# A gated recurrence whose tiles hold both heads of one direction instead of both directions of one head

## The chip, the cores and the metric

The kernel runs on one core of one Trainium2 chip. The metric is the device time of one execution in microseconds (us); lower is better. The engines of a core work side by side, each on its own queue in order: TensorE (PE, with its weight loads shown as PEld), VectorE (DVE), ScalarE (ACT), GpSimd (POOL) and SyncE (SP), which issues most of the DMAs.

## What is computed

The reference is a stack of two two-layer transformer blocks over 512 tokens of width 1024, all in float32. The change touches one mixer of the second block alone, a gated linear recurrence (in both layers). For each of 6 heads with 64 keys and 64 values it runs forwards and backwards over the 512 tokens:

```
f = lb + (1 - lb) * sigmoid(z)          # one gate per key, per direction
k = (1 - lb) * sigmoid(-z)
state = f_t * state + k_t v_t           # forwards with z_fwd, backwards with z_bwd
o = q * state                           # o = o_fwd + o_bwd
```

The other mixers of those layers are a gated convolution of 31 taps and a dilated attention of 6 heads. After them come an output product and a convolutional feed-forward network.

## The kernel before, in words

Tokens lie along the free dimension and channels on the 128 partitions. Every large weight matrix comes in 128x1024 tiles by DMA and is split into a high and a low part (`weight`, L132: a cast on ACT, L129, and a subtraction on DVE, L130). A projection `proj` (L993) is 24 matmuls of 512 columns (`mm3`, L147 to L149) into a bank tagged `d`.

The kernel computes the recurrence without a scan over tokens, as a 512 x 512 matrix of scores for each head, built level by level. `LEVELS` (L937) are block lengths m = 1, 2, 4, ... 256. At level m, a key in one half of a block of 2m tokens meets a query in the other half. Forward scores have the query in the second half, backward scores in the first. Gates are gathered in products that double in length at each level.

In the kernel before, a tile of the recurrence belongs to one head: rows 0 to 63 hold the forward direction and rows 64 to 127 the backward one. There are a gate tile F, a key tile K and a query tile Q for each of the two heads of a pair p (three pairs in a layer). Per head and level:

- `queries` (L1149) multiplies queries by gates on DVE, once for each direction: 64 partitions x 256 elements, into a tile of 512 columns. The other half of the columns was set to zero when the layer began (L991), so that a product over 128 rows sums the two directions with nothing from the wrong half.
- `diagonal` (L1170) handles m up to 64 within 128 x 128 blocks. It makes 8 matmuls (128 rows, 64 output partitions, 64 columns) into one bank, tag `r`. The float32 matmul shows in the trace as two passes, so that 8 matmuls are 16 instructions. A masked copy on DVE (L1186) then picks this level's elements into `AD`; at m = 0 (the diagonal itself) a plain copy on ACT does (L1182), and at m = 64 two copies on ACT (L1189) into `AT`.
- `far` (L1196) handles m = 128 and 256, with 4 matmuls of 128 or 256 columns over 128 rows each, into two `r` tiles in turn, and copies on ACT (L1208, L1215).
- `double` (L1159) extends the products: K on DVE (L1167), then F on POOL (L1168), once for each direction, 64 partitions x 256 elements.

`recurrent` (L1218) runs the levels of the two heads one level apart: head 1 does level i - 1 while head 0 does level i, so there is one step more than there are levels. In pairs 1 and 2 each step also issues two taps of the convolution on DVE (L1022). After the levels come the products with the values (L1250, and L1257 and L1258 for the diagonal blocks, which use 64 rows and 64 output partitions each), a norm and a gate. `recurrent_start` (L1114) makes F, K and Q from the projections. It copies Q for each head and direction on ACT (L1139).

The eight banks of PSUM are `d` 2, `s` 2, `t` 2, `o` 1, `r` 1 (L1281). `s` and `t` belong to the dilated attention's scores and transposes (L328, L1091), `o` to its output and to that of the recurrence.

The steps are traced in the order `MIX_STEPS` (L1271): c0 r0 c1 d0 s1 r1 d1 s2 r2 e d2 (c convolution, r recurrence, d dilated attention, s the start of a recurrence, e the end of the convolution). A scheduler orders each engine's instructions when the program is built, earlier steps first. Later work fills the places where nothing earlier is ready; the order on the chip is then fixed.

Of the kernel before, what the change touches and what calls it, by code (L numbers as in the profile page):

```python
# [17 lines left out]
P = 128  # L18
D = 1024
KC = D // P  # L20
T = 512
# [948 lines left out]
def halves(ap, m):  # L970

    v = ap.rearrange("p (n two m) -> p n two m", two=2, m=m)
    return v[:, :, 0], v[:, :, 1]


class Mixers:


    def __init__(self, b, l, a, at, yp):
        self.b, self.l, self.a, self.at = b, l, a, at  # L980
        self.Y = [b.tile(yp, [P, T], F32, f"Y{k}") for k in range(KC)]
# [132 lines left out]
    def recurrent_start(self, p, pp, tag):  # L1114
# [3 lines left out]
        lb, om = b.lbs[self.l]  # L1118
        self.F, self.K, self.Q = [], [], []
        for h in range(2):  # L1120
            i = 2 * p + h
            pz = self.proj(16 + i)
# [9 lines left out]
        pq = self.proj(13 + p)  # L1132
        qp = b.tile(at, [P, T], F32, "raw")
        nc.scalar.activation(qp, pq, AF.Sigmoid)
        nc.vector.tensor_tensor(qp, qp, pq, op=ALU.mult)
# [12 lines left out]

    def queries(self, m, h):  # L1149
        b, Q, F = self.b, self.Q, self.F  # L1150
        nc = b.nc
        qs = self.qs[m]
# [6 lines left out]
    def double(self, m, h):  # L1159
# [10 lines left out]
    def diagonal(self, h, qs, m):  # L1170

        b, K, AT, AD = self.b, self.K, self.AT, self.AD
# [7 lines left out]
        src = pd.rearrange("p (a b) -> p a b", a=4)  # L1180
        if m == 0:
            nc.scalar.copy(AD[h], src)  # L1182
        elif m < 64:
            mk = b.recmask[:, int(math.log2(m))]
            mk = bass.AP(tensor=mk.tensor, offset=mk.offset, ap=[mk.ap[0], [0, 4], [1, 64]])
            nc.vector.copy_predicated(AD[h], mk, src)  # L1186
        else:
            for s in range(2):
                nc.scalar.copy(self.blocks(h, s, 1 - s), src[64 * s:64 * s + 64])  # L1189

# [4 lines left out]

    def far(self, m, h, qs):  # L1196
        b, K, AT = self.b, self.K, self.AT
        nc = b.nc
        for x in range(2):
            pf = b.tile(self.pp, [P, T], F32, "r")  # L1200
            if m == P:
                for y in range(2):
                    i = 2 * y + x
                    mm = nc.tensor.matmul(pf[:, y * P:(y + 1) * P], K[h][:, i * P:(i + 1) * P],
                                     qs[:, (i ^ 1) * P:((i ^ 1) + 1) * P], start=True, stop=True)
                for y in range(2):
                    i = 2 * y + x
                    nc.scalar.copy(AT[h][:, i, (i ^ 1) * P:((i ^ 1) + 1) * P], pf[:, y * P:(y + 1) * P])  # L1208
            else:
                u = slice(256 * (1 - x), 256 * (1 - x) + 256)  # L1210
                for y in range(2):
                    i = 2 * x + y
                    mm = nc.tensor.matmul(pf[:, 256 * y:256 * y + 256], K[h][:, i * P:(i + 1) * P], qs[:, u], start=True,
                                          stop=True)
                nc.scalar.copy(AT[h][:, 2 * x:2 * x + 2, u], pf.rearrange("p (y t) -> p y t", y=2))  # L1215
        return mm

    def recurrent(self, p):  # L1218
# [4 lines left out]
        self.AD = AD = [b.tile(at, [P, 4, 64], F32, "AD") for _ in range(2)]  # L1223
        for h in range(2):
            self.diagonal(h, self.Q[h], 0)
        levels = LEVELS[::-1]
        for i in range(len(levels) + 1):

            for h in range(2):
                if 0 <= i - h < len(levels):  # L1230
                    m = levels[i - h]
                    qs = self.queries(m, h)
                    if m < P:
                        self.diagonal(h, qs, m)
                    else:
# [39 lines left out]
def mixers(b, l, a, first, env):  # L1275
# [138 lines left out]
def layout(x):  # L1414
# [31 lines left out]

    v["lb_gamma"] = g("lb_gamma_2").reshape(2, 2, 6, 64).transpose(0, 2, 1, 3).reshape(-1)
    o["odd_w_in"] = wtiles(g("odd_w_in")[0])
# [4 lines left out]
    for l in range(2):  # L1453
# [3 lines left out]
        w = g("w_in_2")[l]  # L1457
        z = w[:, 2048:2816].reshape(D, 2, 6, 64).transpose(0, 2, 1, 3).reshape(D, 768)
        o[f"w_in_{l}"] = wtiles(np.concatenate([w[:, :2048], z, w[:, 2816:]], 1))
# [200 lines left out]
```

## Time and profile before

| | us |
|---|---|
| median of 3 runs | 3237.75 (3232.91 to 3242.60) |
| profiled execution, its own time | 3238.63 |
| profiled execution, span of its trace | 3236.6 |
| PE busy in the span | 3059.5 (95%) |
| DVE busy | 2131.1 (66%) |
| ACT busy | 1338.0 (41%) |
| POOL busy | 393.0 (12%) |

The span runs from the first instruction to the last. Busy time is the union of an engine's instructions. The matmuls are pipelined, so a busy PE is not necessarily at its peak. The granted clock of TensorE was 0.983 of full speed on average.

### The profile page before, as it was taken

What the parts mean: (1) busy time and instruction counts of PE and PEld (TensorE: products, weight loads), DVE (VectorE), ACT (ScalarE), POOL (GpSimd) and SP (SyncE); (2) the same over time, 40 slices, a digit from 0 to 9 for tenths busy, and PEclk for the clock granted to TensorE, in tenths of its full rate; (3) what the DMA queues carried; (4) which work ended last, traced back from release to release, by engine and by line L of the source; (5) the groups of instructions that cost most, each with busy time, mean ns of one, the idle gap of its engine ahead of it and who ended that gap; (6) DMA issues with size and microseconds to landing.
All of it is one profiled execution on the core that took longest, in us unless ns stands there. A gap on an engine that the chain in (4) does not pass through costs nothing.

```text
span 3236.6 us, 46233 instructions
## 1 busy us (share of the span) xinstructions
PE 3059.5 (95%) x18168; PEld 2509.2 (78%) x18168; DVE 2131.1 (66%) x3745; ACT 1338.0 (41%) x2343; POOL 393.0 (12%) x434
## 2 busy tenths in 40 slices
PE   7999999999999999899998889899999899899998
PEld 5776888888888777788887666688888666688887
DVE  6656565544457667556657997586766897764545
ACT  4656431221335555432334444542334345543423
POOL 0000100000021111200003332200002422210000
PEclk9999999999999999899999999999999999999999
DMA  6322324434302222156641222246652222323332
GB/s 235 101 75 86 131 86 124 130 124 124 110 22 77 53 59 79 66 163 189 188 156 53 71 74 66 92 134 189 191 176 66 71 80 66 105 74 96 98 96 61
DMA packets 100330, 342.65 MB, mean 106 GB/s; under 512 B 12176, under 2 KB 15888, under 8 KB 97040
## 3 DMA queue, kind: packets, MB, share of 16 engines
q1 hardware_dynamic: 93840, 325.53, 31.7%
q0 software_dynamic: 5120, 11.01, 1.6%
q8 instruction: 143, 2.34, 0.3%
q10 hardware_dynamic: 1152, 3.15, 0.3%
q14 instruction: 75, 0.61, 0.1%
HBM read 326.54 MB, written 2.10 MB: 102 GB/s over the span
## 4 chain that ended last, share of the span: by engine, by line
PE 46%; DVE 15%; ACT 2%; DMA 2%; issue 2%; POOL 0%; DVEq 0%; POOLq 0%; ACTq 0%; SPq 0%
PE dd L148 11%; PE dd L147 11%; PE dd L149 11%; DVE qs L1155 3%; DVE rk L1167 2%; PE d L148 2%; PE d L147 2%; PE d L149 2%; DVE wlo L130 1%; DMA K<-K 1%; PE o L1098 1%; DVE AD L1186 1%; DVE nw L242 1%; DMA wraw<-in_w_ada 1%; PE o L1250 1%
## 5 line engine op out<-in xcount | busy, mean ns | idle before, releaser
L148 PE MATMUL dd<-axl,whi 128*128 128x512 f32 (+1 forms) x2728 | 979.4, 360 | 12.7 <-DVE axl L244 11.3
L147 PE MATMUL dd<-axh,whi 128*128 128x512 f32 (+1 forms) x2728 | 978.9, 360 | 12.6 <-ACT axh L243 12.3
L149 PE MATMUL dd<-axh,wlo 128*128 128x512 f32 (+1 forms) x2728 | 976.9, 359 | 0.0
L129 ACT CAST whi<-wraw 128x1024 fp32r<-128x1024 f32 (+1 forms) x388 | 402.8, 1042 | 1010.7 <-PE dd L148 747.5
L130 DVE TENSOR_TENSOR wlo<-wraw,whi 128x1024 fp32r<-128x1024 f32 (+1 forms) x361 | 444.2, 1234 | 335.8 <-ACT whi L129 326.3
L148 PEld LDWEIGHTS dd<-axl,whi 128*128 128x128 f32 x2728 | 520.2, 191 | 92.1 <-DVE axl L244 14.2
L147 PEld LDWEIGHTS dd<-axh,whi 128*128 128x128 f32 x2728 | 519.9, 191 | 90.5 <-ACT axh L243 14.6
L149 PEld LDWEIGHTS dd<-axh,wlo 128*128 128x128 f32 x2728 | 520.4, 191 | 76.5
L218 POOL TENSOR_TENSOR sq<-sq,sq 128x256 f32<-128x256 f32 x90 | 73.0, 819 | 1851.7 <-ACT sq L213 1788.2
L181 DVE CUSTOM_DVE_ANT_0 adaj<-wraw,cond,vecs 128x1024 bf16<-128x1024 f32 x160 | 205.3, 1283 | 136.5 <-DMA wraw<-in_ada_w 87.1
L147 PE MATMUL d<-axh,whi 128*128 128x512 f32 x664 | 275.3, 415 | 12.0 <-ACT axh L129 9.8
L148 PE MATMUL d<-axl,whi 128*128 128x512 f32 x664 | 273.1, 411 | 1.8 <-DVE axl L130 1.8
L149 PE MATMUL d<-axh,wlo 128*128 128x512 f32 x664 | 270.8, 408 | 1.1 <-DVE wlo L130 1.1
L1168 POOL TENSOR_TENSOR rf<-rf 64x256 f32<-64x256 f32 x192 | 160.4, 835 | 388.2 <-DVE rk L1167 357.1
L154 DVE SCALAR_TENSOR_TENSOR hx<-dd,mod,hx 128x512 f32<-128x512 f32 (+1 forms) x113 | 72.7, 645 | 164.8 <-PE dd L149 164.7
L147 PE MATMUL dd<-ach,whi 128*128 128x256 f32 x568 | 160.7, 283 | 0.0
L148 PE MATMUL dd<-acl,whi 128*128 128x256 f32 x568 | 160.6, 283 | 0.0
L149 PE MATMUL dd<-ach,wlo 128*128 128x256 f32 x568 | 160.5, 282 | 0.0
L147 PEld LDWEIGHTS d<-axh,whi 128*128 128x128 f32 x664 | 126.2, 190 | 41.0 <-ACT axh L129 11.4
L148 PEld LDWEIGHTS d<-axl,whi 128*128 128x128 f32 x664 | 126.3, 190 | 31.6 <-issue 4.9
L149 PEld LDWEIGHTS d<-axh,wlo 128*128 128x128 f32 x664 | 126.4, 190 | 27.5 <-DVE wlo L130 2.3
L328 PE MATMUL s<-K,Q 128*128 128x256 f32 (+1 forms) x336 | 116.4, 357 | 21.8 <-DMA K<-K 13.6
(364 smaller groups left out, 4691.2 us busy)
## 6 DMA issues: line engine op xcount, KB each, us to landing
wraw<-in_mlp_w SPq DMA_DIRECT2D x128, 512.0 KB, 3.5
wraw<-in_w_ada SPq DMA_DIRECT2D x96, 512.0 KB, 4.0
wraw<-in_w_up SPq DMA_DIRECT2D x88, 512.0 KB, 3.5
wraw<-in_w_in SPq DMA_DIRECT2D x56, 512.0 KB, 3.5
wraw<-in_ada_w SPq DMA_DIRECT2D x48, 512.0 KB, 3.6
adaw<-in_ada_wb SPq DMA_DIRECT2D x16, 1024.0 KB, 4.8
wraw<-in_w_down SPq DMA_DIRECT2D x32, 512.0 KB, 3.6
wraw<-in_odd_w_in SPq DMA_DIRECT2D x24, 512.0 KB, 3.6
```

The lines of the kernel that those rows point to most:

```text
L129: self.nc.scalar.copy(hi, src)
L130: (e or self.nc.vector).tensor_tensor(lo, src, f32(hi), op=ALU.subtract)
L147: mm(ps, hi[:, k], xh[:, sl], start=first, stop=False)
L148: mm(ps, hi[:, k], xl[:, sl], start=False, stop=False)
L149: mm(ps, lo[:, k], xh[:, sl], start=False, stop=last)
L154: self.nc.vector.scalar_tensor_tensor(h, ps, gate[:, m:m + 1], h, op0=ALU.mult, op1=ALU.add)
L181: nc.vector.tensor_tensor_reduce(junk, raw, c, 1.0, self.vec(bias)[:, i:i + 1], ALU.mult, ALU.add, out[:, i:i + 1])
L218: e.tensor_tensor(acc, acc, s2, op=ALU.add)
L328: mm(ps, q[:, slot, toks], k1[:, keys], start=True, stop=False)
L1155: nc.vector.tensor_tensor(halves(qs[r], m)[1 - d], halves(Q[h][r], m)[1 - d], halves(F[h][r], m)[1 - d], op=ALU.mult)
L1167: nc.vector.tensor_tensor(k[d], k[d], whole[1 - d], op=ALU.mult)
L1168: nc.gpsimd.tensor_tensor(f[1 - d], f[1 - d], whole[d], op=ALU.mult)
```

## The change

A tile of the recurrence now belongs to one direction d: rows 0 to 63 are head 0, rows 64 to 127 head 1. Queries and doubling are done for both heads at once on 128 partitions. A query tile holds, for each direction, only the 256 columns that have queries, so there is nothing to zero and the tiles for the levels go. Each head's scores come from 64 rows of the array, one product per direction, with the two heads' products next to each other in two banks (`r` and `s`, and at m = 256 also `t` and `o`). At m = 1 to 32 a product has 32 columns. The two heads are no longer one level apart. The projection's output needs no copying to make Q. The weights' columns are reordered on the host.

```diff
-        self.qs = {m: b.tile(at, [P, T], F32, f"qs{m}") for m in LEVELS[::-1]}
-        for qs in self.qs.values():
-            b.nc.gpsimd.memset(qs, 0.0)
...
-        for h in range(2):
-            q = b.tile(at, [P, T], F32, "rq")
-            for d in range(2):
-                nc.scalar.copy(q[64 * d:64 * d + 64], qp[64 * h:64 * h + 64])
-            self.Q.append(q)
+        self.Q = b.tile(at, [P, T], F32, "rq")
+        nc.scalar.activation(self.Q, pq, AF.Sigmoid)
+        nc.vector.tensor_tensor(self.Q, self.Q, pq, op=ALU.mult)
...
+    def queries(self, m):
+        b, nc = self.b, self.b.nc
+        qs = b.tile(self.at, [P, 2, T // 2], F32, "qs")
         for d in range(2):
-            r = slice(64 * d, 64 * d + 64)
-            nc.vector.tensor_tensor(halves(qs[r], m)[1 - d], halves(Q[h][r], m)[1 - d], halves(F[h][r], m)[1 - d],
-                                    op=ALU.mult)
+            o = qs[:, d].rearrange("p (n m) -> p n m", m=m)
+            nc.vector.tensor_tensor(o, halves(self.Q, m)[1 - d], halves(self.F[d], m)[1 - d], op=ALU.mult)
         return qs
...
         for d in range(2):
-            r = slice(64 * d, 64 * d + 64)
-            f, k = halves(self.F[h][r], m), halves(self.K[h][r], m)
+            f, k = halves(self.F[d], m), halves(self.K[d], m)
             e = slice(m - 1, m) if d == 0 else slice(0, 1)
-            whole = [f[i][:, :, e].broadcast_to([64, n, m]) for i in range(2)]
+            whole = [f[i][:, :, e].broadcast_to([P, n, m]) for i in range(2)]
             nc.vector.tensor_tensor(k[d], k[d], whole[1 - d], op=ALU.mult)
             nc.gpsimd.tensor_tensor(f[1 - d], f[1 - d], whole[d], op=ALU.mult)
...
-        pd = b.tile(self.pp, [P, T], F32, "r")[:, :256]
+        pds = [b.tile(self.pp, [P, T], F32, t)[:, :256] for t in "rs"]
+        rows = [slice(64 * h, 64 * h + 64) for h in range(2)]
...
         for i in range(4):
-            for s in range(2):
-                k, q = i * P + 64 * s, i * P + 64 * (1 - s if m == 64 else s)
-                nc.tensor.matmul(pd[64 * s:64 * s + 64, 64 * i:64 * i + 64], K[h][:, k:k + 64], qs[:, q:q + 64], start=True,
-                                 stop=True)
+            for d in range(2):
+                for s in range(2):
+                    k = slice(i * P + 64 * s, i * P + 64 * s + 64)
+                    for h, r in enumerate(rows):
+                        out = pds[h][64 * s:64 * s + 64, 64 * i:64 * i + 64]
+                        if m == 0:
+                            nc.tensor.matmul(out, K[d][r, k], qs[r, k], start=d == 0, stop=d == 1)
+                        else:
+                            o = halves(out, m)[1 - d]
+                            q = qs[r, d, 64 * i + 32 * s:64 * i + 32 * s + 32].rearrange("p (n m) -> p n m", m=m)
+                            nc.tensor.matmul(o, K[d][r, k], q, start=True, stop=True)
...
+        if m == P:
+            pfs = [b.tile(self.pp, [P, T], F32, t) for t in "rs"]
...
+        else:
+            for d in range(2):
+                pfs = [b.tile(self.pp, [P, T], F32, t) for t in ("rs", "to")[d]]
...
-        for i in range(len(levels) + 1):
-
-            for h in range(2):
-                if 0 <= i - h < len(levels):
-                    m = levels[i - h]
-                    qs = self.queries(m, h)
-                    if m < P:
-                        self.diagonal(h, qs, m)
-                    else:
-                        last = self.far(m, h, qs)
-                    if 2 * m < T:
-                        self.double(m, h)
+        self.diagonal(self.Q, 0)
+        for m in LEVELS[::-1]:
+            qs = self.queries(m)
+            if m < P:
+                self.diagonal(qs, m)
+            else:
+                last = self.far(qs, m)
+            if 2 * m < T:
+                self.double(m)
             self.tap(2 if p else 0)
...
-                   "rf": 2, "rk": 2, "rq": 2, "AD": 2, "rg": 1, "nr0": 1, "nt": 1,
+                   "rf": 2, "rk": 2, "rq": 1, "qs": 3, "AD": 2, "rg": 1, "nr0": 1, "nt": 1,
```

At m = 64 the new `diagonal` makes 16 matmuls of 64 columns for both heads and the copies as before. At m = 128 `far` makes 8 matmuls of 128 columns over 64 rows and 4 copies (2 blocks each) in place of 8 of one block. At m = 256 it makes 8 matmuls of 256 columns over 64 rows and the 4 copies as before.

## Rows read from the trace of the kernel before

**Rows 1.** The page: the chain that ended last, by engine.

```profile
PE 46%; DVE 15%; ACT 2%; DMA 2%; issue 2%; POOL 0%; DVEq 0%; POOLq 0%; ACTq 0%; SPq 0%
```

**Rows 2.** Busy time by stretch: the first layer's three recurrences (first; sum).

```profile
1773.90:1838.30 64.40, 54.45 (x435) 40.29 (x435) 60.45 (x105) 19.09 (x35) 30.24 (x36) 0.98 0.20 58
...
sum 193.10, PE 163.67 PEld 117.97 DVE 179.59 ACT 70.55 POOL 86.51; mean PE 54.56 PEld 39.32 DVE 59.86 ACT 23.52 POOL 28.84
```

**Rows 3.** The same, second layer (2522:2586, 2629:2695, 2723:2788).

```profile
sum 195.00, PE 165.36 PEld 118.57 DVE 181.75 ACT 72.45 POOL 86.50; mean PE 55.12 PEld 39.52 DVE 60.58 ACT 24.15 POOL 28.83
```

**Rows 4.** The chain of waits, 1773 to 1840 us: by line.

```profile
by line: DVE qs L1155 27.7%; DVE rk L1167 18.9%; issue 8.2%; DVE cy L1022 8.0%; DVE AD L1186 6.8%; DVE wlo L130 6.1%; PE r L1213 4.2%; POOL rf L1168 3.6%; PE r L1178 2.8%; DVE Q L303 2.5%; DVE K L311 2.4%; PE o L1250 1.9%; PE d L149 1.7%; P
```

**Rows 5.** The timeline of DVE, 1784 to 1793 us: start, length, what.

```profile
1785.31 2.38 DVE L1155 TENSOR_TENSOR qs<-rq,rf 64x256 f32<-64x256 f32 x4
...
1788.33 0.44 DVE L1186 COPY_PREDICATED AD<-recmask,r 128x256 f32<-128x256 uint8 x1
1788.66 0.86 DVE L1167 TENSOR_TENSOR rk<-rk,rf 64x256 f32<-64x256 f32 x2
1789.55 1.64 DVE L130 TENSOR_TENSOR wlo<-wraw,whi 128x1024 fp32r<-128x1024 f32 x1
...
1792.55 0.72 DVE L1155 TENSOR_TENSOR qs<-rq,rf 64x256 f32<-64x256 f32 x1
```

**Rows 6.** Groups by line and shape: count, busy us, mean ns, idle before.

```profile
L130 DVE TENSOR_TENSOR wlo<-wraw,whi 128x1024 fp32r<-128x1024 f32 x345 | 429.0, 1246 | 320.9 <-ACT whi L129 311.4
...
L1168 POOL TENSOR_TENSOR rf<-rf 64x256 f32<-64x256 f32 x192 | 160.4, 835 | 388.2 <-DVE rk L1167 357.1 <-DVE st L1078 14.8 <-DVE st L1080 8.9
...
L218 POOL TENSOR_TENSOR sq<-sq,sq 128x256 f32<-128x256 f32 x90 | 73.0, 819 | 1851.7 <-ACT sq L213 1788.2 <-DMA cond<-in_c 58.6 <-DMA wraw<-in_w_up 3.7
...
L1139 ACT COPY rq<-raw 64x512 f32<-64x512 f32 x24 | 14.8, 619 | 7.1 <-DVE raw L1135 6.8
L218 DVE TENSOR_TENSOR sq<-sq,sq 128x256 f32<-128x256 f32 x36 | 16.3, 453 | 11.7 <-ACT sq L213 10.9
```

**Rows 7.** Line L1155: ns min/median/max, starts, shape.

```profile
L1155 DVE TENSOR_TENSOR qs<-rq,rf x216: 407/423/843, 1763.1 to 2784.8; 64x256 f32<-64x256 f32 x108
```

**Rows 8.** Busy sums of Rows 2's stretches: L1155; L1167; tile r; tile pr.

```profile
sum 193.10, DVE 57.66; mean DVE 19.22
...
sum 193.10, DVE 42.33; mean DVE 14.11
...
sum 193.10, PE 53.91 PEld 42.02 DVE 15.91 ACT 17.05; mean PE 17.97 PEld 14.01 DVE 5.30 ACT 5.68
...
sum 193.10, PE 5.13 PEld 3.40 DVE 14.82 ACT 9.69; mean PE 1.71 PEld 1.14 DVE 4.94 ACT 3.23
```

**Rows 9.** The timeline of PE, 1788.3 to 1791 us: around one burst.

```profile
1788.59 0.39 PE L147 MATMUL d<-axh,whi 128*128 128x512 f32 x1
1788.81 0.40 PE L148 MATMUL d<-axl,whi 128*128 128x512 f32 x1
1789.14 0.69 PE L1178 MATMUL r<-qs,rk 128*64 128x64 f32 x16
1789.75 0.50 PE L149 MATMUL d<-axh,wlo 128*128 128x512 f32 x1
```

**Rows 10.** The timeline of PE, 1842 to 1846 us: tiles of 64 rows.

```profile
1842.88 0.27 PE L1257 MATMUL o<-AD,rV 64*64 64x64 f32 x1
...
1843.36 0.22 PE L1258 MATMUL r<-AD,rV 64*64 64x64 f32 x1
```

**Rows 11.** The timeline of PE, 1820 to 1839 us: the far levels.

```profile
1820.98 0.68 PE L1204 MATMUL r<-qs,rk 128*128 128x128 f32 x4 [0.92 <-DVE qs L1155]
...
1825.64 1.02 PE L1213 MATMUL r<-qs,rk 128*128 128x256 f32 x4
...
1834.88 1.10 PE L1213 MATMUL r<-qs,rk 128*128 128x256 f32 x4 [2.94 <-DVE qs L1155]
```

**Rows 12.** Busy sum outside Rows 2: 1838.3:1882, 1945.7:1975.3, 2040.3:2065.

```profile
sum 98.00, PE 91.95 PEld 63.87 DVE 73.22 ACT 68.53 POOL 0.00; mean PE 30.65 PEld 21.29 DVE 24.41 ACT 22.84 POOL 0.00
```

More of the change, by code (lines that the diff above doesn't have):

```diff
@@ L1118, in recurrent_start @@
         lb, om = b.lbs[self.l]
-        self.F, self.K, self.Q = [], [], []
-        for h in range(2):
-            i = 2 * p + h
+        self.F, self.K = [], []
+        for d in range(2):
+            i = 2 * p + d
             pz = self.proj(16 + i)
@@ L1145, in recurrent_start, with double @@
         b.values(pp, self.V, raw, 4, tag)
[L1149 to L1152, printed above, removed]
+    def queries(self, m):
+        b, nc = self.b, self.b.nc
+        qs = b.tile(self.at, [P, 2, T // 2], F32, "qs")
         for d in range(2):
[L1154 to L1156 removed]
+            o = qs[:, d].rearrange("p (n m) -> p n m", m=m)
+            nc.vector.tensor_tensor(o, halves(self.Q, m)[1 - d], halves(self.F[d], m)[1 - d], op=ALU.mult)
         return qs
[L1159 removed]
+    def double(self, m):
         nc = self.b.nc
@@ new lines, in diagonal @@
+        rows = [slice(64 * h, 64 * h + 64) for h in range(2)]
+        if m == 64:
+            for i in range(4):
+                for s in range(2):
+                    for h, r in enumerate(rows):
+                        nc.tensor.matmul(pds[h][64 * s:64 * s + 64, 64 * i:64 * i + 64],
+                                         K[s][r, i * P + 64 * s:i * P + 64 * s + 64], qs[r, s, 64 * i:64 * i + 64],
+                                         start=True, stop=True)
+            for h in range(2):
+                src = pds[h].rearrange("p (a b) -> p a b", a=4)
+                for s in range(2):
+                    nc.scalar.copy(self.blocks(h, s, 1 - s), src[64 * s:64 * s + 64])
+            return
@@ new lines, in diagonal @@
+        for i in range(4):
+            for d in range(2):
+                for s in range(2):
+                    k = slice(i * P + 64 * s, i * P + 64 * s + 64)
+                    for h, r in enumerate(rows):
+                        out = pds[h][64 * s:64 * s + 64, 64 * i:64 * i + 64]
[5 more added lines that the diff above has]
+                            nc.tensor.matmul(o, K[d][r, k], q, start=True, stop=True)
@@ L1191, in blocks @@
+        for h in range(2):
+            src = pds[h].rearrange("p (a b) -> p a b", a=4)
+            if m == 0:
+                nc.scalar.copy(AD[h], src)
+            else:
+                mk = b.recmask[:, int(math.log2(m))]
+                mk = bass.AP(tensor=mk.tensor, offset=mk.offset, ap=[mk.ap[0], [0, 4], [1, 64]])
+                nc.vector.copy_predicated(AD[h], mk, src)
     def blocks(self, h, s, c):
@@ L1194, in blocks, with far @@
         return bass.AP(tensor=v.tensor, offset=v.offset + 64 * c, ap=[v.ap[0], [T + P, 4], [1, 64]])
-    def far(self, m, h, qs):
+    def far(self, qs, m):
         b, K, AT = self.b, self.K, self.AT
         nc = b.nc
-        for x in range(2):
-            pf = b.tile(self.pp, [P, T], F32, "r")
-            if m == P:
+        rows = [slice(64 * h, 64 * h + 64) for h in range(2)]
+        if m == P:
+            pfs = [b.tile(self.pp, [P, T], F32, t) for t in "rs"]
+            for d in range(2):
@@ L1202, in far @@
                 for y in range(2):
-                    i = 2 * y + x
-                    mm = nc.tensor.matmul(pf[:, y * P:(y + 1) * P], K[h][:, i * P:(i + 1) * P],
-                                     qs[:, (i ^ 1) * P:((i ^ 1) + 1) * P], start=True, stop=True)
-                for y in range(2):
[L1207 to L1215, printed above, removed]
+                    i = 2 * y + d
@@ new lines, in far @@
+                    for h, r in enumerate(rows):
+                        mm = nc.tensor.matmul(pfs[h][:, (2 * d + y) * P:(2 * d + y + 1) * P], K[d][r, i * P:(i + 1) * P],
+                                              qs[r, d, y * P:(y + 1) * P], start=True, stop=True)
+            for h in range(2):
+                for d in range(2):
+                    v = AT[h].rearrange("p a b -> p (a b)")
+                    v = bass.AP(tensor=v.tensor, offset=v.offset + d * T + (1 - d) * P,
+                                ap=[v.ap[0], [2 * (T + P), 2], [1, P]])
+                    nc.scalar.copy(v, pfs[h][:, 2 * d * P:2 * (d + 1) * P].rearrange("p (y q) -> p y q", y=2))
+        else:
+            for d in range(2):
+                pfs = [b.tile(self.pp, [P, T], F32, t) for t in ("rs", "to")[d]]
+                for y in range(2):
+                    i = 2 * d + y
+                    for h, r in enumerate(rows):
+                        mm = nc.tensor.matmul(pfs[h][:, 256 * y:256 * y + 256], K[d][r, i * P:(i + 1) * P], qs[r, d],
+                                              start=True, stop=True)
+                for h in range(2):
+                    nc.scalar.copy(AT[h][:, 2 * d:2 * d + 2, 256 * (1 - d):256 * (1 - d) + 256],
+                                   pfs[h].rearrange("p (y t) -> p y t", y=2))
@@ L1223, in recurrent @@
         self.AD = AD = [b.tile(at, [P, 4, 64], F32, "AD") for _ in range(2)]
-        for h in range(2):
-            self.diagonal(h, self.Q[h], 0)
-        levels = LEVELS[::-1]
-        for i in range(len(levels) + 1):
-            for h in range(2):
-                if 0 <= i - h < len(levels):
-                    m = levels[i - h]
-                    qs = self.queries(m, h)
-                    if m < P:
-                        self.diagonal(h, qs, m)
-                    else:
-                        last = self.far(m, h, qs)
-                    if 2 * m < T:
-                        self.double(m, h)
+        self.diagonal(self.Q, 0)
[3 more added lines that the diff above has]
+                self.diagonal(qs, m)
+            else:
+                last = self.far(qs, m)
+            if 2 * m < T:
+                self.double(m)
             self.tap(2 if p else 0)
```

20 lines of the change are left out of this document (4 added, 16 removed).

## The prediction, made before the change was run

> **What bounds the kernel now.** I began with the whole page: PE holds 46% of the chain that ended last and DVE only 15% [rows 1]. That average mixes stages, so I cut the trace into the stretches in which a recurrence runs. The first layer has three, 193.1 us in all. DVE is busy in 179.6 us of it (93%), PE in 163.7 us (85%) [rows 2]; the second layer shows the same, 181.8 of 195.0 us [rows 3]. In the first stretch the chain of waits runs over DVE: the queries hold 27.7% of it, the keys' doubling 18.9%, the masked copies 6.8%; the recurrence's matmuls hold about 6% [rows 4]. So these 388 us of the kernel hang on DVE. PE's far levels even wait for the queries, once for 2.94 us [rows 11].
>
> One level of both heads shows how the time is made up. From one group of queries to the next are 7.24 us (1785.31 to 1792.55), and DVE hardly pauses: four queries 2.38 us, two masked copies of 0.44, four doublings in two pairs of 0.86, and work from outside the recurrence, here a weight split of 1.64 us [rows 5]. The mean is 64.4 us / 9 levels = 7.15 us with all that surrounds them [rows 2].
>
> **What the change takes from DVE and POOL.** Queries and doublings go from four instructions of 64 partitions a level to two of 128. Partitions cost nothing: an addition on DVE over 128 x 256 takes 453 ns, the doubling on POOL over 64 x 256 835 ns and a POOL addition over 128 x 256 819 ns [rows 6]. The work therefore halves. Per layer 57.7 us of queries and 42.3 us of doubling [rows 8] lose 28.8 + 21.2 = 50.0 us of DVE time, 100 us in both layers. POOL's doubling loses 80 of 160.4 us [rows 6]. The ACT copies of Q, 14.8 us in 24 instructions [rows 6], go; four of the six starts lie in mid-mixer, where I count two of the four copies each as on the path: 4 x 2 x 0.62 = 5 us. POOL's zeroing at the layers' starts lies beside the norm before, and I count nothing for it; without that cover it would be worth some us more.
>
> **What it does to PE.** A burst of 16 passes (8 float32 matmuls) takes 0.69 us, the last pass itself 0.22: 31 ns a pass [rows 9]. The two heads make 32 passes a level, 1.0 us. Products of 64 rows and 64 output partitions stand already in the kernel: 32 passes of 64 columns start within 0.48 us, 15 ns a pass [rows 10], so four quarters of the array do run side by side. After the change a level m = 1 to 32 has 64 passes of 32 columns, a shape that the trace doesn't show. Bounds: 7.5 ns a pass if it goes by columns (0.5 us a level), 31 ns if the row halves don't overlap (2.0 us). I take the 64-column price of the nearest row, 15.5 ns: 1.0 us, no gain. The Trainium skill's TensorEngine Tiling (Array Packing), Instruction Overhead, has a rule against halving the columns: some 60 cycles of overhead a matmul, so that short products cost as those of 60 columns. By that rule the term is 1.0 us a level, by columns alone 0.5; no run here shows 32 columns yet.
>
> The rest of PE, per recurrence: m = 0 has 64 passes, 1.0 us as now. m = 64 has 32 passes, 0.5 for 1.0 us. At m = 128 sixteen passes of 135 ns ((0.68 - 0.27) / 3, [rows 11]) become sixteen half-height ones, in pairs 1.1 for 2.2 us. At m = 256, 214 ns a pass ((1.02 - 0.38) / 3, [rows 11]), 1.7 for 3.4 us. Sum now 1 + 7 + 2.2 + 3.4 = 13.6, after 1 + 6 + 0.5 + 1.1 + 1.7 = 10.3 us: 3.3 us less. A burst costs about 0.1 us going in (0.33 between starts where 0.22 is usual) and as much coming out [rows 9]. Sixteen bursts become eight and two or three in the far levels: 1 us less. Together some 4 us of PE a recurrence, 25 us in all, but PE is not what a phase waits for, so it counts as room for other work.
>
> **The level after the change.** With one group for both heads, no second head covers the first's waits. Adding up the chain: last query 0.42 [rows 7]; 0.1 to PE (estimate); the end of a running matmul and the switch 0.3 [rows 9]; 64 passes, 1.0 + 0.22 [rows 10]; two masked copies, 0.33 apart, 0.7 [rows 5]; first doubling 0.43 and 0.12 to POOL; two POOL instructions, 1.6 to 1.7 [rows 6]; 0.1 back to DVE. That is 5.1 us. DVE's work a level is 0.7 + 0.86 + 1.19 = 2.75 us, and the outside work of about 2 us that now runs in a level (7.15 x 0.93 - 4.8) makes 4.75. Chain and work are close, and an outside instruction that has just begun holds the chain up; I add half of one (0.5 us) and take 5.6 us. A phase is then 2.5 (m = 0) + 8 x 5.6 + 4.5 (m = 256, no doubling behind it; both ends are estimates from the same pieces) = 51.8 against 64.4 us: 12.6 us less, six times 76 us. The step that the stagger adds goes with it.
>
> **What is given back.** In a layer's phases PE has 163.7 - 53.9 = 109.8 us of other work [rows 2, 8]. In 155 us, at the same share and with 40 us for the recurrence, it finds 92; at 95% it finds 107. So 3 to 18 us move out, to stretches where PE reads 92.0 busy of 98.0 us [rows 12]. I take 9 us a layer. The new score tiles also take a bank of tag `s` at each level and `t` and `o` at the last. The dilated attention, which now runs its softmax inside the phases of pairs 1 and 2 (14.8 us of DVE and 5.1 of PE a layer on tile pr, [rows 8]), may have to wait for them. What is late next is then its transposes and its sum behind the recurrence. Nothing to 15 us a layer; I take 4, as the recurrence holds the bank only until the masked copy. New waits on the query tile cost nothing: three buffers, and a level reads one.
>
> **Sum.** 76 + 5 - 2 x 9 - 2 x 4 = 55 us off the profiled execution's own 3238.6 us (span 3236.6, 2 us around it, and 0.9 us over the median): 3184 us.
>
> **Rivals.** (a) *DVE and POOL hinder each other, and it remains.* A query alone takes 0.42 us, beside POOL 0.72, at most 0.84 [rows 5, 7]; a weight split 1.64 where the mean is 1.25 [rows 5, 6]. In the new level DVE has only outside work while POOL doubles. If that work is kept out of those 1.6 us, only the other 1.6 us (PE's burst and the switch) is left for 2.0 us of it, and each level grows by 0.4 us: 6 x 8 x 0.4 = 19 us, 3203 us. SBUF — State Buffer (Trainium skill), Who interferes with whom, states a harder form: a DVE instruction with two SBUF inputs and a GpSimd one that reads SBUF exclude each other for the whole instruction. By that rule the added time goes to the remaining POOL time; the rows' stretch of 0.3 to 0.4 us, less than POOL's 0.8, only partly bears it out.
>
> (b) *Full relief.* Phases stay as full of DVE as now and nothing moves out: (193.1 - 129.6 / 0.93) = 54 us a layer, with 5 us for Q: 3238.6 - 108 - 5 = 3126 us. For it speaks the 93%; against it the chain of 5.1 us.
>
> (c) *It doesn't do what it says:* the halves don't run side by side. Then a level has 2.0 us of passes: 6 x 1.0 + 1.0 + 0.5 + 1.1 + 1.7 = 10.3 us a recurrence in the chain, 62 us: 3246 us, no change. Rows 10 speak against.
>
> (d) *Slower: the unstaggered chain.* The orders on DVE and PE are fixed; if at each level the chain stands behind a whole weight split on DVE (1.64 us) and PE's waits last some 0.8 us more, a level is 5.1 + 1.6 + 0.8 = 7.5 us, and a phase 2.5 + 60 + 4.5 = 67 us, 2.6 more than now. No PE work moves out then, but the dilated attention's 8 us stay, and the 5 for Q: 3239 + 6 x 2.6 + 8 - 5 = 3258 us. It decides from a level of about (64.4 - 7) / 8 = 7.2 us on. For it: PE waits now for the queries although a second head runs; against: DVE's work a level falls to 4.75 us.
>
> **How the numbers follow.** Forecast 0.50 (own range 3150 to 3215), (a) 0.13, (b) 0.15, (c) 0.08, (d) 0.14. The range takes in (b) and (c), with the bound of 7.5 ns a pass (18 us less) and of the work moved out: 3115 to 3252; (d) stays out. A change under 0.3% (10 us) can't be told from none here. Faster: nearly all of the forecast, of (a) and of (b), 0.76; within 0.3%: most of (c) and a little of the others, 0.10; slower 0.14.
>
> **What would show it.** In the trace after: 108 queries and 96 doublings on DVE at about 0.42 to 0.6 us, POOL's about 0.8. The starts of successive query groups lie 5 to 6 us apart, and the six phases last about 52 us each. The bursts of 64 passes take about 1.2 us. DVE's share in the phases falls below 93%, and the stretches outside them grow by 10 to 15 us a layer. It is wrong if a level still takes over 7 us, if bursts take over 2 us, or if dilated scores first start after the last level and the tail grows by what the phases lost.

## The result, and the profile after

The changed kernel takes 3179.4 us (median of 4 runs, 3177.9 to 3180.5) against 3238.2 us before (median of 4 runs): a ratio of 0.9823, 95% interval 0.9809 to 0.9837, or 59 us less. 3184 us was forecast. The profiled execution's span is 3178.1 us against 3236.6.

The page after, its PE, DVE, ACT and POOL line and the chain by engine, answers to [rows 1]:

```profile
PE 3041.3 (96%) x19512; PEld 2500.7 (79%) x19512; DVE 2005.8 (63%) x3541; ACT 1313.7 (41%) x2292; POOL 293.8 (9%) x320
...
PE 49%; DVE 11%; DMA 3%; ACT 2%; issue 2%; POOL 1%; DVEq 0%; POOLq 0%; ACTq 0%; SPq 0%
```

DVE fell from 2131 to 2006 us of busy time, POOL from 393 to 294, PE from 3060 to 3041. In the chain DVE went from 15% to 11% and PE from 46% to 49%.

Where the time went is seen by stretches. Here are the three recurrences of the first layer (columns: stretch, length, busy us of PE, PEld, DVE, ACT and POOL with their instructions, granted clock, share of the DMA engines, GB/s). They answer to [rows 2]. The first begins with head 0's burst of m = 1; its m = 0 and head 1's burst of m = 1 had run before (1763 to 1767 us). The first stretch of [rows 2] begins with m = 0, 3.0 us ahead of its first burst of m = 1 (1776.9 us), so cut alike the three phases differ by some 3 us less:

```profile
1777.50:1820.00 42.50, 38.29 (x533) 28.71 (x533) 41.44 (x72) 13.56 (x24) 13.09 (x16) 1.00 0.18 52
1873.60:1911.50 37.90, 34.66 (x605) 25.39 (x604) 24.73 (x53) 12.18 (x23) 10.54 (x16) 1.00 0.14 43
1959.50:1999.70 40.20, 36.97 (x613) 26.06 (x614) 23.12 (x50) 12.83 (x24) 10.54 (x16) 1.00 0.14 41
sum 120.60, PE 109.92 PEld 80.17 DVE 89.29 ACT 38.58 POOL 34.17; mean PE 36.64 PEld 26.72 DVE 29.76 ACT 12.86 POOL 11.39
```

193.1 us became 120.6, three phases of about 40 us where 51.8 were forecast. DVE is full in the first alone (98%); in the other two it is busy 65% and 58%. So the second and the third phase are no longer bound by DVE's work. The rest of that layer's mixers (from the first gate to the last output of a mixer) answers to [rows 12], which leaves out the stretch before the first phase. Of the changed kernel the three longer pieces and the sum of all four (the first is 1756.4:1777.5):

```profile
1820.00:1873.60 53.60, 52.80 (x291) 38.18 (x289) 50.27 (x102) 32.89 (x52) 2.10 (x4) 1.00 0.37 108
1911.50:1959.50 48.00, 47.85 (x271) 34.73 (x271) 25.58 (x62) 26.65 (x48) 2.10 (x4) 1.00 0.38 110
1999.70:2037.70 38.00, 34.51 (x196) 23.31 (x193) 26.15 (x65) 27.79 (x50) 2.10 (x4) 0.91 0.42 118
sum 160.70, PE 155.05 PEld 113.09 DVE 110.91 ACT 95.39 POOL 6.31; mean PE 38.76 PEld 28.27 DVE 27.73 ACT 23.85 POOL 1.58
```

And the sum of the same four pieces of the kernel before (1754.4:1773.9, 1838.3:1882, 1945.7:1975.3, 2040.3:2063):

```profile
sum 115.50, PE 108.80 PEld 78.17 DVE 80.82 ACT 76.50 POOL 0.00; mean PE 27.20 PEld 19.54 DVE 20.20 ACT 19.12 POOL 0.00
```

So 72.5 us were won in the phases and 45.2 were lost outside them: 27.3 us a layer. (With the 3 us of the cut above it is some 70 and 42, and the difference is the same.) In the second layer the mixers take 281 us (2473.9 to 2755.2, from the second gate on) against 309 us (2502.2 to 2811.2). Both layers make 55 of the 58.5 us.

What moved out is told by the tiles that the projections write. First the sum over the three phases before, tile `d`, then after, tiles `d` and `pr` (the dilated attention's softmax):

```profile
sum 193.10, PE 105.04 PEld 65.45 DVE 3.44 ACT 8.77; mean PE 35.01 PEld 21.82 DVE 1.15 ACT 2.92
```

```profile
sum 120.60, PE 67.22 PEld 42.74 DVE 3.42 ACT 5.29; mean PE 22.41 PEld 14.25 DVE 1.14 ACT 1.76
...
sum 120.60, PE 0.00 PEld 0.00 DVE 0.00 ACT 0.00; mean PE 0.00 PEld 0.00 DVE 0.00 ACT 0.00
```

374 instructions of projections in the phases became 246: 128 fewer of 0.23 us are 29 us of PE that run outside now. The softmax, with 14.8 us of DVE and 5.1 of PE in the phases before [rows 8], has left them altogether.

One level after the change, on DVE, in the second recurrence. The level runs from the second query at 1884.05 to the one at 1888.18, 4.13 us, where two heads needed 7.24 in the level of [rows 5]:

```profile
1884.05 0.43 DVE L1146 TENSOR_TENSOR qs<-rq,rf 128x256 f32<-128x256 f32 x1 [0.51 <-POOL rf L1157]
1885.64 0.43 DVE L1156 TENSOR_TENSOR rk<-rk,rf 128x256 f32<-128x256 f32 x1 [1.17 <-PE s L1189]
1885.99 0.44 DVE L1197 COPY_PREDICATED AD<-recmask,r 128x256 f32<-128x256 uint8 x1
1886.32 0.44 DVE L1197 COPY_PREDICATED AD<-recmask,s 128x256 f32<-128x256 uint8 x1
1886.65 0.57 DVE L1156 TENSOR_TENSOR rk<-rk,rf 128x256 f32<-128x256 f32 x1
1887.15 0.41 DVE L1146 TENSOR_TENSOR qs<-rq,rf 128x256 f32<-128x256 f32 x1
1888.18 0.42 DVE L1146 TENSOR_TENSOR qs<-rq,rf 128x256 f32<-128x256 f32 x1 [0.62 <-POOL rf L1157]
```

The two POOL instructions between them:

```profile
1886.21 0.73 POOL L1157 TENSOR_TENSOR rf<-rf 128x256 f32<-128x256 f32 x1 [2.20 <-DVE rk L1156]
1887.37 0.78 POOL L1157 TENSOR_TENSOR rf<-rf 128x256 f32<-128x256 f32 x1 [0.43 <-DVE rk L1156]
```

From the end of the last query (1884.48) to the first doubling (1885.64) are 1.16 us. The first doubling runs ahead of the masked copies, and the second behind them. DVE then waits 0.62 us for POOL. Over seven levels the mean, from one group of queries to the next, is 4.0 us in the second phase (1879.25 to 1907.07) and in the third, and 5.05 us in the first (1779.92 to 1815.28), where DVE is full; before the change it was 6.6 to 6.9 us in all three. The groups, which answer to [rows 6 and 7]:

```profile
L1157 POOL TENSOR_TENSOR rf<-rf 128x256 f32<-128x256 f32 x96 | 69.6, 732 | 389.1 <-DVE rk L1156 389.1
...
L1146 DVE TENSOR_TENSOR qs<-rq,rf 128x256 f32<-128x256 f32 x108 | 51.1, 490 | 18.4 <-POOL rf L1157 18.1
...
L1156 DVE TENSOR_TENSOR rk<-rk,rf 128x256 f32<-128x256 f32 x96 | 41.7, 449 | 24.7 <-PE s L1189 21.3 <-PE s L1215 2.3 <-PE s L1170 0.7
```

The instructions are half as many, on twice the partitions. A query's mean is 490 ns where it was 561 (120.4 us busy before, 51.1 now), a doubling's 449 where it was 441, POOL's 732 where it was 835.

Five starts of a burst of 32-column passes on PE, as one round of four quarters and the next begin (start, length, what):

```profile
1782.51 0.22 PE L1189 MATMUL r<-qs,rk 64*64 64x32 f32 x1
1782.51 0.22 PE L1189 MATMUL s<-qs,rk 64*64 64x32 f32 x1
1782.52 0.22 PE L1189 MATMUL r<-qs,rk 64*64 64x32 f32 x1
1782.53 0.22 PE L1189 MATMUL s<-qs,rk 64*64 64x32 f32 x1
1782.57 0.22 PE L1189 MATMUL r<-qs,rk 64*64 64x32 f32 x1
```

A round of four passes takes 58 ns over a whole burst, so a pass takes 15 ns, as with 64 columns [rows 10]. Halving the columns brought nothing on PE: 64 passes take 0.93 us, not the 0.5 that columns alone give. The Trainium skill's TensorEngine Tiling (Array Packing), Instruction Overhead, has a matmul of 1 column take as long as one of 60; the trace agrees with it for 32 columns against 64.

### The profile page after: what moved, and what is told of

Same layout as the page of the kernel before. It is cut to its first block, busy times and chain, and to the rows that moved or that the text cites. A ratio compares the mean times of both kernels' runs of the same rounds, so it can differ in the third digit from the quotient of the medians.

```text
span 3178.1 us, 48476 instructions
## 1 busy us (share of the span) xinstructions
PE 3041.3 (96%) x19512; PEld 2500.7 (79%) x19512; DVE 2005.8 (63%) x3541; ACT 1313.7 (41%) x2292; POOL 293.8 (9%) x320
## 4 chain that ended last, share of the span: by engine, by line
PE 49%; DVE 11%; DMA 3%; ACT 2%; issue 2%; POOL 1%; DVEq 0%; POOLq 0%; ACTq 0%; SPq 0%
PE dd L148 12%; PE dd L147 11%; PE dd L149 11%; PE d L148 2%; PE d L147 2%; PE d L149 2%; DVE cy L1018 1%; DMA K<-K 1%; DVE wlo L130 1%; PE o L1094 1%; DVE nw L242 1%; DVE qs L1146 1%; DMA dbias<-in_dilated 1%; DVE axl L244 1%; DMA wraw<-in_w_ada 1%
## 5 line engine op out<-in xcount | busy, mean ns | idle before, releaser
L148 PEld LDWEIGHTS dd<-axl,whi 128*128 128x128 f32 x2728 | 520.4, 191 | 93.4 <-DVE axl L244 14.8
L329 PE MATMUL s<-K,Q 128*128 128x512 f32 (+1 forms) x336 | 108.9, 339 | 1.0 <-DMA K<-K 1.0
```

Source lines behind the costliest of these rows:

```text
L148: mm(ps, hi[:, k], xl[:, sl], start=False, stop=False)
L329: mm(ps, q[:, slot, toks], k2[:, keys], start=False, stop=mask is None)
```

## The experiments

All times are medians, with the ratio to runs of the kernel before on the same chip (its medians there were 3236.0 to 3236.9 us).

### 1. DVE and POOL as many instructions as before

```diff
-            nc.vector.tensor_tensor(o, halves(self.Q, m)[1 - d], halves(self.F[d], m)[1 - d], op=ALU.mult)
+            for h in range(2):
+                r = slice(64 * h, 64 * h + 64)
...
+                nc.vector.tensor_tensor(o, halves(self.Q[r], m)[1 - d], halves(self.F[d][r], m)[1 - d], op=ALU.mult)
```

and the same for both instructions of `double`.

> The changed kernel with its PE work and its banks, but each query and each doubling instruction on DVE and POOL cut into two of 64 partitions, one for each head: as many instructions on DVE and POOL as before the change. Theory (the phases hung on DVE, and the halved DVE work is the gain): DVE has 100 us more and a level's chain grows by two doublings, a query and two POOL instructions (0.43 x 2 + 0.42 + 1.6 = 2.9 us on 4.6 us), so most or all of the gain goes: 3220 to 3290 us. Rival (the products in row halves are the gain): PE is as after the change, so it stays within 3180 to 3200 us.

Measured: 3274.1 us, ratio 1.0117 (1.0096 to 1.0138), slower than before the change. Its three recurrences of the first layer:

```profile
1779.00:1834.00 55.00, 50.54 (x534) 37.13 (x534) 50.58 (x87) 13.30 (x22) 22.76 (x30) 0.84 0.14 43
1886.00:1948.50 62.50, 54.39 (x650) 39.94 (x649) 58.95 (x101) 15.16 (x27) 26.41 (x36) 0.93 0.19 53
1989.00:2051.00 62.00, 55.42 (x639) 41.07 (x639) 53.05 (x95) 17.45 (x31) 26.23 (x36) 0.84 0.16 44
```

They last 55 to 62 us and DVE is full again (92%, 94%, 86%). The chain of waits, 1773 to 1840 us, shows the doubling and the queries at its head, as in [rows 4]:

```profile
by line: DVE rk L1160 20.5%; DVE qs L1148 16.7%; PE d L149 8.9%; PE d L148 7.9%; PE d L147 7.8%; DVE cy L1018 5.4%; PE r L1193 5.0%; DVE AD L1201 4.2%; PE o L1266 4.1%; issue 3.9%; PE o L1233 3.0%; DVE wlo L130 2.4%; PE s L1193 2.3%; PE r L
```

The product layout alone, with DVE's old work and without the stagger, loses 36 us. Its phases (179.5 us) are not longer than those of the kernel before (193.1), so part of the loss lies outside them. One caution: the granted clock in these stretches is 0.84, 0.93 and 0.84, against 1.00 after the change. In the mixers as a whole it is 0.90 in the first layer (1758.9 to 2091.1 us) and 0.93 in the second (2522.8 to 2859), against 0.99 in both after the change. If PE had been the bound throughout, that would be 332 x 0.09 + 336 x 0.06 = 50 us; so of the 95 us against the changed kernel at least 45 are DVE's, POOL's and the chain's.

### 2. The two heads one after the other on PE

```diff
-        for i in range(4):
-            for d in range(2):
-                for s in range(2):
+        for h, r in enumerate(rows):
+            for i in range(4):
+                for d in range(2):
+                    for s in range(2):
```

and so at m = 64, 128 and 256.

> The changed kernel with the same products, but all of head 0's before all of head 1's in each burst, so that neighbours use the same row half. Theory (two row halves run side by side, and PE is now the bound of these stages): a pass goes from 15 to about 31 ns; 10.3 us a recurrence, of which most shows: 3179 + 40 to 62 = 3220 to 3241 us. Rival (PE has room, or row halves make no difference): less than 15 us, 3179 to 3194 us.

Measured: 3212.3 us, ratio 0.9928 (0.9913 to 0.9943), 33 us over the changed kernel. It lies between the two, and below the 40 us that the theory asked for. One head's run of 22 passes:

```profile
1788.35 0.83 PE L1189 MATMUL r<-qs,rk 64*64 64x32 f32 x22
```

(0.83 - 0.22) / 21 = 29 ns a pass against 15: the row halves do run side by side when neighbours alternate. But the run takes away only a part of the overlap. In the order as built, the first eight passes of a burst and the seam between the two heads still alternate, two passes of one head and two of the other (from 1788.96 to 1789.16 us here), and PE's busy time, 3041.3 us after the change, grows far less than the 62 us that the theory counted:

```profile
PE 3072.2 (96%) x19512; PEld 2532.3 (79%) x19512; DVE 2021.7 (63%) x3541; ACT 1309.0 (41%) x2288; POOL 295.8 (9%) x320
```

So 31 us of PE's time were added and the kernel takes 33 us more: what is added to PE shows in full. The 62 us were too many, as the run leaves a part of the overlap; that PE bounds these stages agrees with it.

### 3. Another bank for the second head

```diff
-        pds = [b.tile(self.pp, [P, T], F32, t)[:, :256] for t in "rs"]
+        pds = [b.tile(self.pp, [P, T], F32, t)[:, :256] for t in "rt"]
```

and `rt`, `so` in the far levels.

> The changed kernel with the second head's scores in a bank of tag t in place of s (and s in place of t at m = 256). Theory (the dilated attention's scores wait for the recurrence's s tiles, which moves its softmax behind the phases and costs time there): scores start within the phases of pairs 1 and 2 again, 8 to 25 us less: 3154 to 3171 us. Rival (PE is full whatever the order, so what moves is work without a price): 3174 to 3184 us.

Measured: 3175.3 us, ratio 0.9813 (0.9798 to 0.9828). Its interval overlaps that of the changed kernel. The first scores of the second pair's attention still come behind the recurrence (at 1921.6 us; the last query of that phase ends at 1910.6). The copies that complete its keys (`K<-K`, L313) are issued at 1908.5 to 1911.6 us, as the phase ends. So the bank `s` isn't what keeps the attention out of the phases; they are over before it is ready. In the kernel before, the same scores began at 1920.1 us, inside a phase that lasted until 1945.7. The theory fell, and the time lies in the rival's range.

### 4. The kernel before with half of DVE's and POOL's recurrence work

```diff
-        for d in range(2):
+        for d in range(1):
             r = slice(64 * d, 64 * d + 64)
             nc.vector.tensor_tensor(halves(qs[r], m)[1 - d], halves(Q[h][r], m)[1 - d], halves(F[h][r], m)[1 - d],
```

and so in `double`.

> The kernel before the change, whose queries and doublings are done for the forward direction alone: the backward halves are left out of the computation. DVE and POOL then have the instruction counts of the changed kernel, PE, the stagger and the banks are as before the change. Theory (DVE bound the phases): 3238 us falls by at least as much as the change won, to 3130 to 3190 us. Rival (PE's new products won it): PE is as before, 3215 to 3240 us.

Measured: 3173.6 us, ratio 0.9806 (0.9789 to 0.9822): 63 us less, with PE's products, the stagger and the banks of the kernel before. The sum over its three phases in the first layer (1772.9:1818.5, 1872:1916.5, 1957:2001):

```profile
sum 134.10, PE 131.33 PEld 94.76 DVE 101.96 ACT 50.09 POOL 47.15; mean PE 43.78 PEld 31.59 DVE 33.99 ACT 16.70 POOL 15.71
```

134 us where 193 were: DVE's and POOL's relief alone brings what the whole change brought (the intervals overlap). All else that the change does, PE's new products, the banks, the lost stagger and the copies of Q, comes to nothing that shows in sum; single terms of opposite sign are not excluded. The new products are what lets the kernel have the relief and compute both directions. Two things are to be kept in mind. DVE's and POOL's halves were not taken away one at a time; that it is DVE's goes by [rows 4], where POOL holds 3.6% of the chain. And these phases are 13.5 us longer than the changed kernel's although the whole takes the same time, so the length of the phases by itself is not what the time follows.

### 5 to 8. Winning back what was given back

After the change the chain between the second and the third recurrence (1911 to 1960 us) holds a new wait:

```profile
by line: PE d L149 16.7%; PE d L147 15.7%; DMA dbias<-in_dilated 15.2%; PE d L148 14.9%; PE o L1262 7.3%; DVE pr L1073 6.4%; PE o L1094 5.6%; issue 4.4%; PE t L1087 3.4%; ACT whi L129 2.1%; PE o L1277 1.8%; DVE Y L1280 1.4%; PE o L1229 1.3%
```

The bias tiles' loads, which nothing waited for before, are 15% of it. Experiment 5 gives them buffers (`"dbias": 6` in place of 2).

> The changed kernel with six buffers in place of two for the bias tiles of the dilated attention. After the change the chain between the second and the third recurrence waits for those loads (7.4 us of 48 in the first layer), as all softmaxes now come in a row behind the recurrence. Theory (part of what was given back is this new wait): the loads run during the recurrence and the stretches behind the recurrences shorten by 3 to 7 us each, 10 to 30 us in all: 3150 to 3169 us. Rival (PE has enough other work there): 3174 to 3184 us.

Measured: 3179.8 us, ratio 0.9828 (0.9811 to 0.9845). No gain, although the wait is gone from the same stretch:

```profile
by line: PE d L147 17.8%; PE d L149 17.6%; PE d L148 16.9%; PE o L1094 11.3%; PE t L1087 8.7%; PE o L1262 7.3%; PE s L328 4.3%; PE s L329 3.8%; PE o L1229 2.1%; PE o L1277 1.8%; PE t L1229 1.4%; POOL rf L1157 1.3%; PE o L1269 1.2%; PE r L12
```

PE's projections took its place in the chain. Experiment 6 puts the masked copies behind the doubling:

```diff
+            take = None
             if m < P:
-                self.diagonal(qs, m)
+                take = self.diagonal(qs, m)
...
             if 2 * m < T:
                 self.double(m)
+            if take:
+                take()
```

> The changed kernel with the two masked copies of a level put behind the doubling in the program, off the chain from the matmuls to the next queries. Theory (in the phases of pairs 1 and 2 the chain of a level and no longer DVE's work sets the period, DVE is busy 58 to 65% there): the period falls by up to 0.66 us, the phase from 38 to about 33 us; but the time gains little of it, since the other work only moves out: 3160 to 3180 us. Rival (the period is set by DVE's work): phases stay at 37 to 40 us and the time at 3174 to 3184 us.

Measured: 3180.9 us, ratio 0.9833 (0.9813 to 0.9853). The first phase shortens from 42.5 to 36.0 us, and the stretch behind it grows from 53.6 to 59.5:

```profile
1777.50:1813.50 36.00, 33.04 (x513) 24.91 (x512) 35.16 (x66) 11.08 (x20) 11.23 (x16) 1.00 0.19 52
1813.50:1873.00 59.50, 57.90 (x317) 42.15 (x315) 55.76 (x109) 32.62 (x54) 2.11 (x4) 1.00 0.35 99
```

In the second and third phase the queries span 37.2 and 37.6 us, as after the change (37.5 and 38.0), which the theory had wrong. What it had right is that a shorter phase no longer shortens the kernel; the time lies in the rival's range. Experiment 7 is the three edits together, experiment 8 the same with a third buffer for raw weights.

> The changed kernel with bank t for the second head, six bias buffers and the masked copies last together. Theory: the bias buffers' gain shows, the other two add a few us: 3140 to 3165 us. Rival (PE is the bound throughout): 3170 to 3180 us.

> As the run with the three together, with three raw weight buffers in place of two in the mixers, so that a projection's weights can be loaded one tile further ahead. Theory (projections wait for their weights' split on ACT and DVE, not for the load): no difference to that run, within 4 us. Rival (the load is late): 5 to 20 us less.

Measured: 3185.8 us, ratio 0.9846 (0.9828 to 0.9864), and 3189.8 us, 0.9860 (0.9840 to 0.9879). Neither gains. Experiment 7 lies above both of its ranges, and experiment 8 within 4 us of it, as its theory had it; the interval of 8 lies above that of the changed kernel, so the three edits with the third buffer lose some 10 us.

### 9 and 10. Less PE work, after and before

```diff
-        b.mm3(ps, w, self.a)
+        hi, lo = w
+        for k in range(KC):
+            xh, xl = self.a[k]
+            b.nc.tensor.matmul(ps, hi[:, k], xh, start=k == 0, stop=False)
+            b.nc.tensor.matmul(ps, hi[:, k], xl, start=False, stop=k == KC - 1)
```

> The changed kernel without the third product (low part of the weights) of the 24 mixer projections of each layer that go through proj; the split on DVE stays. That is 24 x 8 matmuls of 0.23 us, 44 us of PE a layer, 87 in all. Theory (PE now sets the time of the mixers, so the shorter phases only moved work): 55 to 87 us less than 3179, 3092 to 3124 us. Rival (chains of waits set it): under 35 us, 3144 to 3179 us.

> The kernel before the change without the same product: again 87 us of PE less. Theory (in the recurrences DVE sets the time, outside them PE does for the most part): only the outside gains, 20 to 50 us less than 3237, 3187 to 3217 us, clearly less than the same edit brings the changed kernel. Rival (PE was the bound before as well): as much as with the changed kernel, 55 to 87 us.

Measured: the changed kernel 3129.0 us, ratio 0.9665 (0.9650 to 0.9679), 50 us under the changed kernel; the kernel before 3195.9 us, ratio 0.9873 (0.9858 to 0.9887), 41 us under itself. The first lies between the theory (55 and more) and its rival, the second within the 20 to 50 us of its theory. But both ran at a lower granted clock in the mixers. Here are the two layers' mixers, from the first gate to the last output of a mixer, of experiment 9 and then of 10 (the clock stands behind the engines' busy times):

```profile
1762.00:2016.40 254.40, 229.25 (x2514) 164.65 (x2514) 205.66 (x423) 139.62 (x234) 46.39 (x60) 0.95 0.33 95
2447.80:2708.70 260.90, 232.65 (x2535) 167.32 (x2534) 203.82 (x415) 139.58 (x234) 46.41 (x60) 0.94 0.31 88
...
1754.00:2047.10 293.10, 241.64 (x1838) 172.67 (x1838) 261.34 (x525) 148.26 (x257) 85.41 (x108) 0.91 0.28 85
2479.80:2773.60 293.80, 243.51 (x1859) 174.40 (x1858) 260.84 (x517) 147.98 (x257) 90.70 (x121) 0.91 0.27 80
```

Cut alike, it is 0.99 in both layers of the changed kernel and of the kernel before. If PE had been the bound throughout, the lower clock would have taken back 254 x 0.04 + 261 x 0.05 = 23 us in 9 and 587 x 0.08 = 47 us in 10. So at least 50 of the 87 us show after the change, and PE is most of the bound there. Whether PE's work counts for less in the kernel before can't be read from the pair: 47% of the 87 us against 58% isn't "clearly less", and the clock could make up the whole difference.

### 11 and 12. Another order of the steps

```diff
-MIX_STEPS = "c0 r0 c1 d0 s1 r1 d1 s2 r2 e d2"
+MIX_STEPS = "c0 r0 c1 s1 r1 d0 s2 r2 d1 e d2"
```

for 11, with the output product's order to match; `c0 r0 c1 s1 d0 r1 s2 d1 r2 e d2` for 12.

> The changed kernel with the steps in the order c0 r0 c1 s1 r1 d0 s2 r2 d1 e d2 (and the output product's order to match), so that dilated attention of an earlier pair fills the next recurrence. Theory (the work that was pushed out fills PE's and DVE's gaps in the phases again): 5 to 20 us less, 3159 to 3174 us. Rival (PE is full, or the last step's tail grows): 3175 to 3195 us.

> The changed kernel with each recurrence's start put ahead of the dilated attention before it (c0 r0 c1 s1 d0 r1 s2 d1 r2 e d2): projections of the next pair come first, the attention stays before the recurrence. Theory: PE keeps the same work, so within 8 us of 3179 us. Rival (starts that come early let the next recurrence's levels run beside the attention): 10 to 25 us less.

Measured: 3183.7 us, ratio 0.9834 (0.9819 to 0.9849), no gain, and inside the rival's range; and 3223.5 us, ratio 0.9963 (0.9950 to 0.9975), 44 us over the changed kernel with the same work on every engine. Both sides had the second wrong. Its phases are not where the time goes. Cut from the first burst of m = 2 to the last of m = 256, the first layer's three take 105.2 us (1785.82:1825, 1891.51:1924.9, 1989.33:2022) against 102.2 after the change (1780.48:1819.6, 1879.87:1911.5, 1965.76:1997.2), and about as much of the projections runs inside them, as the sums for tile `d` show, of experiment 12 first:

```profile
sum 105.24, PE 59.34 PEld 38.72 DVE 2.72 ACT 6.44; mean PE 19.78 PEld 12.91 DVE 0.91 ACT 2.15
...
sum 102.19, PE 60.59 PEld 38.35 DVE 2.73 ACT 4.13; mean PE 20.20 PEld 12.79 DVE 0.91 ACT 1.38
```

What differs is outside. The bursts of m = 0 and m = 1 of pair 1 are spread from 1866.7 to 1887.3 us, where they stand within 4 us after the change. And the granted clock is 0.97 and 0.95 in the two layers' mixers (1761.8:2059.4 and 2493.7:2797) against 0.99, which can account for at most 298 x 0.02 + 303 x 0.04 = 18 of the 44 us. The rest is not explained by these runs.

## Why the prediction was right

**What bounds it.** Right: DVE's work in the phases was the bound. Experiment 4 takes away half of that work, and of POOL's, and gets 63 us; experiment 1 puts it back into the changed kernel and loses 95, of which at least 45 are not the lower clock's.

**DVE and POOL halve at no cost for the partitions.** Right: 449 and 732 ns an instruction, and the queries' mean even fell. That they are stretched less beside POOL would fit, but was not tested. DVE's 205.0 us of queries and doublings (120.4 + 84.6) became 92.8 (51.1 + 41.7): 112 us less, where 100 were counted.

**PE.** Right in its main term: 15 ns a pass, four quarters at once, no gain from 32 columns. That row halves don't overlap, rival (c), fell with these 15 ns; experiment 2, which takes a part of the overlap away, has 29 ns in a run of one head and takes 33 us more. PE's busy time fell by 18 us where 25 were counted.

**The level.** Wrong in size: 5.6 us was the forecast, 4.0 us is the mean level in the second and third phase and 5.05 in the first. The step that failed is the chain of 5.1 us. It put the whole burst and both masked copies between the last query and the first doubling, 0.1 + 0.3 + 1.22 + 0.7 = 2.3 us, where 1.16 us were measured: the first 8 passes of a burst, of the first direction, run before the second query is done (at 1883.77 us, the query at 1884.05), the other 56 start 0.2 us behind it and take about 1.0 us, and the first doubling doesn't wait for the copies. The second does, and so POOL's second instruction starts 0.43 us after the end of its first. POOL's pair took 1.51 us, close to the 1.6 that was counted, and 1.94 with that wait. And the half of an outside instruction that was added hardly stands there, since DVE has few of them in the second and third phase. The phases won 72.5 us a layer in place of 38.

**What is given back.** Mis-sized the other way: 45 us a layer in place of 13, beyond both bounds together (18 and 15). Of PE's work 29 us moved out, not 9, and the dilated softmax left altogether, not because of the bank `s` (experiment 3) but because the phases end before it is ready. That is one of the prediction's own signs of being wrong, and it came in part: the scores first start after the last level, and the stretches outside grow by more than half of what the phases lost. This and the level's error nearly cancel: 27.3 us a layer against 25 + 2.5 forecast. The total was right by two errors of some 30 us a layer each, and not by the sizes of its terms; that they cancelled so closely was luck.

**The rivals.** (a), that DVE and POOL still hinder each other, is visible but small: the queries' mean is 490 ns where the median is 418, which makes 108 x 0.072 = 8 us in all. (The 18 us that queries wait for POOL are waits for its results, a part of the chain.) (b), full relief, was nearer than the forecast in the phases' sum (139 us against 155; 120.6 measured), but not in that nothing moves out. (d), the unstaggered chain, needs a level of 7.2 us; even experiment 1, without the stagger and with the old DVE work, has 6.8 us in the second and third phase (1895.89 to 1943.50 in the second, over seven levels). It is slower than before all the same, with a lower clock and a part of the loss outside the phases.

**What stays open.** After the change PE's work is most of what sets the mixers' time: PE time that is added shows in full (31 us of busy time, 33 us, experiment 2), and of 87 us taken away at least 50 show (9). A shorter chain shows nothing (5 and 6). Why the order of the steps moves 44 us (12) is open, and so is why the granted clock fell in experiments 1, 9, 10 and 12. No run with the same work made the mixers clearly faster than the changed kernel; the 4 us of experiment 3 lie within the intervals.

## What to carry to other kernels

When an engine is full with instructions that use half the partitions, putting two independent problems on the two halves halves its work, and the price on TensorE can be nil if the products of the two halves alternate (here they went to different banks; one bank for both was not tried). Before counting a shortened phase as time won, list what other work ran inside it: here some 45 of 72 us came back as work that lost its cover. And a forecast that comes out right in its sum should be checked term by term.

## What the runs showed of the hardware

Float32 passes in quarters of the array (64 rows, 64 output partitions) took 15 ns each with 64 columns and with 32, as long as neighbouring passes went round all four quarters; with passes of one row half alone, column halves in turn, 29 ns. In experiment 1 the granted clock averaged 0.84 in a stretch in which PE reads as busy in 50.5 of 55 us, so part of it ran at 1.2 GHz; the same passes at a like share of busy time (38.3 of 42.5 us) kept 1.00 after the change. With a product of the projections left out, the kernel before went from 0.99 to 0.91 in its mixers and the changed kernel from 0.99 to 0.95 and 0.94. Why is not shown by these runs.
